# A two-block network on one core: where the 2 KB tiles lie in memory, and how early the first layer's sums of squares are issued

## The chip, the cores and the metric

One core of one Trainium2 chip runs the whole program. The metric is the device time of one execution in microseconds; the runs of the kernel before gave 2714.94 us as their median (2714.61 to 2717.44, 3 runs).

## The reference

The input x has 512 tokens of 1024 features. Two blocks are computed one after the other, both of two layers, all in float32. Cut to what matters:

```python
for l in range(2):                                   # first block
    h = _rmsnorm(x, g_mix[l])                        # over the 1024 features
    p = h @ w_in[l]                                  # 384 + 256 + 32 + 2*512 columns
    ...                                              # latent attention of 8 heads, from p[:, :672]
    a, gt = split(p[..., 672:]); u = a * sigmoid(gt)
    u = silu(layernorm(dwconv31(u)))                 # depthwise, 31 taps, 512 channels
    x = x + concat([y_attn, u]) @ w_o[l]
    z = dwconv3(_rmsnorm(x, g_ffn[l]) @ w_up[l])     # 2 * 2816 columns
    zg, zv = split(z); x = x + (silu(zg) * zv) @ w_down[l]
x = _rmsnorm(x, g_final)
for i in range(2):                                   # second block
    mix = ssd_mixer(x) if i == 0 else hgrn2_mixer(x)
    h = layer_norm(ALPHA * x + mix)
    h = layer_norm(ALPHA * h + relu(h @ mlp_w1[i]) ** 2 @ mlp_w2[i])    # 4096 hidden
    x = h + sigmoid(h @ ple_w_gate[i]) * (p[i] @ ple_w_proj[i])
```

## The kernel before, in words

**Tiling.** Everything is kept with features on the 128 partitions and the 512 tokens along the row, so a float32 tile of [128, 512] is 2 KB in each partition. A dense product is done in float32r with both operands split in a high and a low part: `dense` (L722) issues for each of the 8 blocks of 128 features three matmuls (`mm3`, L717: high x high, high x low, low x high) of 128 x 128 weights with 512 columns of activations (256 where the tokens are cut in halves). Of a matmul's operands the activations are the moving one and the weights the stationary one; all of them are tiles of class s. Weights come from HBM in units of 512 KB to tiles of class r, in the order in which they are used, issued by SP; `weights` (L689) has them split by a cast to the high part (ScalarE or VectorE) and a subtraction to the low part (GpSimd or VectorE). psum has 8 banks of one [128, 512] result each.

**The order.** Nothing is issued while the program is recorded. `Recorder.add` (L408) keeps each operation; `Recorder.schedule` (L464) then places all 19111 of them by a list scheduler with costs of its own, and gives every tile a slot. At each step it takes the operation that can start earliest; between those that can start at once, the smallest `prio` (L481), which is the operation's bias, minus a share of the work behind it, plus its place in the recording. So a bias of 300 lets an operation pass as if it stood 300 places later. The classes of slots and their numbers are in `SLOTS` (L617): 86 of class s, of 2 KB each, 12 of t (512 bytes), 24 of n (up to 128 bytes), 4 of u (2168 bytes at most), 3 of r (4 KB), one each of V (per-channel vectors) and C (constants).

**The addresses.** `Recorder.issue` (L589) goes through the operations in order. The first use of a slot makes a tile in the one SBUF pool (`alloc` in `build`, L1655), and the pool lays tiles one behind the other in the order in which they are made. The first lies at byte 16512 of the partition. Since t, u, n, r, V and C tiles are made between the s tiles, these do not all begin at the same place modulo 512 bytes. In the built program they begin, modulo 512, at

| s tiles | modulo 512 | modulo 256 |
|---|---|---|
| s0 to s22 | 448 | 192 |
| s23 to s44 | 64 | 64 |
| s45, s46 | 96 | 96 |
| s47 to s52 | 128 | 128 |
| s53 | 192 | 192 |
| s54 to s85 | 320 | 64 |

A block of 128 columns of weights in such a tile begins at a multiple of 512 bytes within it.

**The start.** `mixer1` (L905) begins the first layer: `gained` (L773) makes from each of the eight X tiles a high part, scaled (ScalarE), and a low part (VectorE); `sumsq` (L747) squares the same eight tiles (ScalarE) and adds the squares up in two sums (`other`: VectorE or GpSimd); `tok_sum` (L731) adds over the partitions by four matmuls with a column of ones from C; `rstd` (L760) reads that (VectorE) and takes the power -0.5 (GpSimd); `spread` (L767) brings it to all partitions by four transposes, and ScalarE copies it to Rb. Each of the eight products for the convolution is read out of its bank by a multiplication with Rb. The five products of the latents are read without Rb. The bias of the sums is set at L908.

Of the kernel before, what the change touches and what calls it, by code (L numbers as in the profile page):

```python
# [9 lines left out]
F32 = mybir.dt.float32  # L10
# [7 lines left out]
P = 128  # L18
S = 512
# [222 lines left out]
class Ap:  # L242
# [55 lines left out]
    def build(self):  # L298
        x = self.tl.real
        for s in self.steps:  # L300
            if s[0] == "i":
                x = x[s[1]]
            elif s[0] == "r":
                x = x.rearrange(s[1], **s[2])
            elif s[0] == "u":
                x = x.unsqueeze(s[1])
            else:
                x = x.to_broadcast(s[1])
        return x
# [307 lines left out]
SLOTS = {"psum": 8, "r": 3, "s": 86, "u": 4, "t": 12, "n": 24, "V": 1, "C": 1}  # L617
KEEP = {"psum": 2, "s": 18, "u": 2, "t": 6, "n": 16}
SIDE_TAPS = 14
EARLY = 3  # L620
FILL = {"mlp0": [(0, 0)], "mlp1": [(1, 0)]}
FULL = (slice(0, S),)
# [3 lines left out]
def record(R, xT, pos, wts, vecs, consts, pT, outT, dbg=None, stop=None):  # L626
    def tl(shape=(P, S), dt=F32, cls=None):
        b = int(np.prod(shape[1:])) * 4
        cls = cls or ("n" if b <= 128 else "t" if b <= 512 else "s")
        assert cls != "s" or b <= 2048  # L630
        return R.tile(cls, shape, dt)

    def bank():
        return R.tile("psum", (P, S), F32)
# [9 lines left out]
    def vec(name, i=0):  # L644
        o, k = vlay[name]
        return V[:, o + i:o + i + 1]
# [42 lines left out]
    def weights(name, l=None):  # L689

        i = used[0]
        u = units[i]
        assert u[0] == name and (l is None or u[1] == l), (u, name, l)
        used[0] += 1
        c, nk = unit_cols(u), u[3]
        if i not in ahead:
            prefetch(i)
        raw = ahead.pop(i)
        rows, per = [], S // c
        for k in range(0, nk, per):  # L700
            m = min(per, nk - k)
            hi, lo = tl((P, m * c), F32R), tl((P, m * c), F32R)
            src = raw[:, k * c:(k + m) * c]
            copy(hi, src)
            R.either.tensor_sub(lo, src, hi)
            rows += [(hi[:, i * c:(i + 1) * c], lo[:, i * c:(i + 1) * c]) for i in range(m)]
        return rows
# [39 lines left out]
    def sumsq(srcs, sl=slice(0, S), both=True, turned=True):  # L747
        accs = []
        for i, s in enumerate(srcs):
            t = tl()  # L750
            R.scalar.activation(t[:, sl], s[:, sl], AF.Square)
            if i < (2 if both else 1):
                accs.append(t)
            elif both and i % 2:
                R.either.tensor_add(accs[1][:, sl], accs[1][:, sl], t[:, sl])
            else:
                R.other.tensor_add(accs[0][:, sl], accs[0][:, sl], t[:, sl])
        return tok_sum(accs, sl, turned)

    def rstd(ps, n, eps, k=4):  # L760
        v = tl((P, k))
        R.vector.tensor_scalar(v, ps[:, 0:k], 1.0 / n, eps, op0=ALU.mult, op1=ALU.add)
        r = tl((P, k))
        R.gpsimd.tensor_tensor(r, v, nh[:, 0:k], op=ALU.pow)
        return r
# [7 lines left out]
    def gained(name):  # L773

        op = []
        for k in range(KD):
            hi, lo = pair()
            R.scalar.activation(hi, X[k], AF.Identity, scale=vec(name, k))
            R.vector.scalar_tensor_tensor(lo, X[k], vec(name, k), hi, op0=ALU.mult, op1=ALU.subtract)
            op.append((hi, lo))  # L780
        return op
# [123 lines left out]
    def mixer1(l):  # L905
        R.label = f"in{l}"
        op = gained(f"g_mix{l}")
        R.bias = 0  # L908
        r = rstd(sumsq(X, turned=False), D, EPS1)
        R.bias = 0  # L910
        Rb = tl()
# [88 lines left out]
        def conv_tile(j):  # L1000
            R.label, R.bias = f"conv{l}", 100
            acc = bank()
            for k in range(CONV_K - SIDE_TAPS):
                wc = vec(f"w_dw_conv{l}", j * CONV_K + k)
# [4 lines left out]
            side = None  # L1009
            for k in range(CONV_K - SIDE_TAPS, CONV_K):  # L1010
                t = tl()
# [141 lines left out]
    def ssd(op):  # L1153
# [69 lines left out]
        def inputs(g):  # L1223
# [3 lines left out]
            if g == 0:  # L1227
                ws, ps = [weights("ssd_w_in_2") for _ in range(EARLY)], [bank() for _ in range(EARLY)]
                for sl in HALVES:
# [404 lines left out]
    for l in range(DEPTH):  # L1634
        mixer1(l)
        dump(f"mix{l}", X)
        if stop == f"mix{l}":
            return
        op = ffn1(l)
        dump(f"ffn{l}" if l == 0 else "b1", X)  # L1640
        if stop == f"ffn{l}":
            return
# [12 lines left out]
def build(tc, xT, pos, wts, vecs, consts, pT, outT, dbg=None, stop=None):  # L1655
    R = Recorder()
    record(R, xT, pos, wts, vecs, consts, pT, outT, dbg, stop)
    R.schedule(SLOTS, KEEP)
    with tc.manual_schedule(), tc.tile_pool(name="sbuf", bufs=1) as sb, \
            tc.tile_pool(name="psum", bufs=1, space=bass.MemoryType.PSUM) as ps:  # L1660
        
        def alloc(t):
            pool = ps if t.cls == "psum" else sb
            name = f"{t.cls}{t.slot}"
            return pool.tile(list(t.shape), t.dt, tag=name, name=name, bufs=1)
        R.issue(tc.nc, alloc)
    return R

# [28 lines left out]
```

## Time and profile before

| | |
|---|---|
| median of 3 runs | 2714.94 us |
| profiled execution, its own time | 2715.32 us |
| span of the profiled execution | 2713.5 us |
| mean granted TensorE clock | 0.993 |
| busy: TensorE, its weight loads | 98%, 82% |
| busy: VectorE, ScalarE, GpSimd | 70%, 44%, 31% |
| moved from HBM | 230 MB |

The span goes from the first to the last instruction; the execution's own time has 1.8 us more around it. In the rows PE is TensorE's matmul, PEld its weight load, DVE VectorE, ACT ScalarE, POOL GpSimd, SP the engine that issues the DMAs. A matmul's busy time is its life in the pipeline, and lives overlap: the step from one to the next is told by starts. All recorded operations have one line (L599, in `issue`), so that rows are told apart by tiles; buffer numbers are left out of them.

### The profile page before, as it was taken

How to read it: one execution, taken by the hardware profiler on the slowest of the kernel's cores; microseconds unless marked ns; L12 is line 12 of the kernel's file. 1: busy time of each engine (PE TensorE's matmuls, PEld its weight loads, DVE VectorE, ACT ScalarE, POOL GpSimd, SP SyncE). 2: the span in 40 equal slices, each digit the busy share in tenths (PEclk: the TensorE clock that was granted, in tenths of full speed). 3: DMA queues.
4: the chain of work that ended last, by engine and by line, in shares of the span. 5: the costliest groups of instructions: out<-in, count | busy, mean ns of one | idle time of the engine just before them, and what ended most of it. 6: DMA issues, size and time to landing. Idle time of an engine off the chain costs nothing.

```text
span 2713.5 us, 38992 instructions
## 1 busy us (share of the span) xinstructions
PE 2671.4 (98%) x15094; PEld 2212.1 (82%) x15094; DVE 1898.9 (70%) x3222; ACT 1200.9 (44%) x2206; POOL 834.2 (31%) x691
## 2 busy tenths in 40 slices
PE   9999999999999999999999999999999999999999
PEld 7777888888778888888778888888988789888889
DVE  8997676678976666685887675555688787554546
ACT  5874333346764323343664432222367674322223
POOL 3561011235721111232441432232412233223332
PEclk8999999999999999999999999999999999999999
DMA  4123132230131223321113412232231123322320
GB/s 164 35 71 116 63 112 98 101 109 29 59 112 62 86 93 109 110 80 63 51 36 109 148 55 103 87 106 97 73 105 48 64 74 107 107 100 89 109 94 32
DMA packets 69449, 235.00 MB, mean 87 GB/s; under 512 B 7824, under 2 KB 11152, under 8 KB 69264
## 3 DMA queue, kind: packets, MB, share of 16 engines
q1 hardware_dynamic: 69264, 232.51, 25.3%
q8 instruction: 119, 1.95, 0.3%
q14 instruction: 66, 0.54, 0.1%
HBM read 230.38 MB, written 2.10 MB: 86 GB/s over the span
## 4 chain that ended last, share of the span: by engine, by line
PE 91%; DVE 6%; issue 1%; ACT 1%; POOL 0%; DMA 0%; SPq 0%; POOLq 0%; ACTq 0%; DVEq 0%
PE psum L599 91%; DVE s L599 5%; DVE psum L599 1%; ACT s L599 1%; DVE n L599 0%; POOL s L599 0%; DMA s<-xT 0%; DVE u L599 0%; SPq L599 0%; POOLq L599 0%; ACTq L599 0%; DVEq L599 0%
## 5 line engine op out<-in xcount | busy, mean ns | idle before, releaser
L599 PE MATMUL psum<-s,s 128*128 128x512 f32 (+4 forms) x12992 | 2608.2, 365 | 23.9 <-DVE s L599 14.7
L599 PEld LDWEIGHTS psum<-s,s 128*128 128x128 f32 (+2 forms) x12992 | 2116.1, 185 | 459.7 <-issue 23.2
L599 POOL TENSOR_TENSOR s<-r,s 128x512 fp32r<-128x512 f32 (+1 forms) x363 | 502.8, 1400 | 1092.5 <-ACT s L599 819.7
L599 ACT CAST s<-r 128x512 fp32r<-128x512 f32 (+1 forms) x743 | 420.6, 612 | 386.4 <-DMA r<-wts 375.4
L599 DVE TENSOR_TENSOR s<-s,s 128x512 f32<-128x512 f32 (+5 forms) x605 | 415.1, 707 | 68.4 <-ACT s L599 57.6
L599 POOL TENSOR_TENSOR s<-s,s 128x512 f32<-128x512 f32 (+5 forms) x234 | 273.0, 1179 | 539.9 <-ACT s L599 290.4
L599 DVE TENSOR_TENSOR s<-s,psum 128x512 f32<-128x512 f32 (+2 forms) x400 | 225.3, 591 | 266.9 <-PE psum L599 265.3
L599 DVE TENSOR_TENSOR s<-r,s 128x512 fp32r<-128x512 f32 x506 | 401.6, 820 | 5.3 <-ACT s L599 2.7
L599 ACT ACTIVATE s<-s 128x512 f32<-128x512 f32 (+1 forms) x335 | 186.2, 578 | 243.7 <-DVE s L599 240.2
L599 ACT ACTIVATE s<-u,V 128x512 f32<-128x512 f32 x200 | 143.0, 761 | 270.4 <-DVE u L599 270.0
L599 ACT ACTIVATE s<-psum 128x512 f32<-128x512 f32 (+2 forms) x176 | 91.9, 524 | 344.5 <-PE psum L599 342.6
L599 DVE SCALAR_TENSOR_TENSOR s<-u,V,s 128x512 f32<-128x512 f32 x176 | 145.9, 830 | 49.0 <-ACT s L599 47.2
L599 DVE SCALAR_TENSOR_TENSOR s<-psum,s 128x512 f32<-128x512 f32 (+1 forms) x88 | 55.7, 640 | 105.0 <-ACT s L599 104.7
L599 DVE TENSOR_TENSOR u<-psum,s 128x512 f32<-128x512 f32 x88 | 60.7, 690 | 92.3 <-PE psum L599 90.3
L599 ACT COPY s<-psum 128x512 f32<-128x512 f32 (+5 forms) x162 | 76.0, 503 | 79.2 <-PE psum L599 77.8
L599 ACT CAST s<-s 128x512 fp32r<-128x512 f32 (+2 forms) x123 | 72.0, 591 | 74.7 <-DVE s L599 67.5
L599 ACT ACT_TABLE_LOAD x72 | 92.4, 1283 | 8.7 <-DVE s L599 6.8
L599 DVE SCALAR_TENSOR_TENSOR psum<-u,V,psum 128x512 f32<-128x512 f32 x128 | 91.8, 743 | 0.3
L599 PE MATMUL psum<-C,s 128*128 128x128 f32 (+1 forms) x532 | 84.9, 272 | 4.5 <-ACT s L599 3.0
L599 DVE SCALAR_TENSOR_TENSOR s<-psum,V,s 128x511 f32<-128x511 f32 (+4 forms) x90 | 65.5, 743 | 29.8 <-ACT s L599 20.7
L599 PEld LDWEIGHTS psum<-C,s 128*128 128x128 f32 x532 | 67.3, 150 | 20.0 <-ACT s L599 7.2
L599 DVE CAST s<-r 128x512 fp32r<-128x512 f32 (+1 forms) x126 | 56.0, 455 | 39.0 <-DMA r<-wts 38.1
(87 smaller groups left out, 834.7 us busy)
## 6 DMA issues: line engine op xcount, KB each, us to landing
r<-wts SPq DMA_DIRECT2D x415, 512.0 KB, 3.5
r<-wts SPq DMA_DIRECT2D x12, 256.0 KB, 2.6
r<-wts SPq DMA_DIRECT2D x8, 384.0 KB, 3.0
s<-xT SPq DMA_DIRECT2D x8, 256.0 KB, 6.1
s<-pT SPq DMA_DIRECT2D x8, 256.0 KB, 3.0
outT<-s SPq DMA_DIRECT2D x16, 128.0 KB, 1.8
r<-wts SPq DMA_DIRECT2D x9, 128.0 KB, 2.0
V<-vecs SPq DMA_DIRECT2D x1, 479.0 KB, 6.7
```

What stands on the lines that cost most here:

```text
L599: getattr(eng, meth)(*[res(a) for a in args], **{k: res(v) for k, v in kw.items()})
```

## The change

It does two things. Before anything is issued, `build` makes all 86 s tiles one behind the other, after a pad of 480 bytes, so that the first begins at 16992 and all of them at 96 modulo 512 (and 96 modulo 256). The other classes come behind them. And in the first layer the sums of squares in front of the mixer are recorded with a bias of 300 in place of 0.

```diff
--- before.py
+++ after.py
@@ -617,6 +617,7 @@
 SLOTS = {"psum": 8, "r": 3, "s": 86, "u": 4, "t": 12, "n": 24, "V": 1, "C": 1}
 KEEP = {"psum": 2, "s": 18, "u": 2, "t": 6, "n": 16}
 SIDE_TAPS = 14
+FIRST = 16512
 EARLY = 3
 FILL = {"mlp0": [(0, 0)], "mlp1": [(1, 0)]}
 FULL = (slice(0, S),)
@@ -905,7 +906,7 @@
     def mixer1(l):
         R.label = f"in{l}"
         op = gained(f"g_mix{l}")
-        R.bias = 0
+        R.bias = 300 if l == 0 else 0
         r = rstd(sumsq(X, turned=False), D, EPS1)
         R.bias = 0
         Rb = tl()
@@ -1663,6 +1664,12 @@
             pool = ps if t.cls == "psum" else sb
             name = f"{t.cls}{t.slot}"
             return pool.tile(list(t.shape), t.dt, tag=name, name=name, bufs=1)
+
+        pad = (96 - FIRST) % 512
+        if pad:
+            sb.tile([P, pad // 4], F32, tag="pad", name="pad", bufs=1)
+        for n in range(SLOTS["s"]):
+            sb.tile([P, S], F32, tag=f"s{n}", name=f"s{n}", bufs=1)
         R.issue(tc.nc, alloc)
     return R
 
```

Where the instructions stand: the schedule differs in the first layer's mixer and what surrounds it; from within the first layer's feed-forward part on, the operations stand in the same order on every engine, in other slots. The names below have the slot ahead of the underscore; the numbers behind it count tiles as they are made, and differ between the two programs.

VectorE at the start, where the low parts of X (SCALAR_TENSOR_TENSOR with V) and the adds of squares (TENSOR_TENSOR of s and s) are made; before:

```order
L599 SCALAR_TENSOR_TENSOR s19_144<-s6_114,V0_65,s16_138 128x512
L599 TENSOR_TENSOR s4_110<-s4_110,s18_142 128x512
L599 TENSOR_TENSOR s14_134<-s14_134,s21_149 128x512
L599 SCALAR_TENSOR_TENSOR s24_164<-s8_118,V0_65,s22_153 128x512
L599 TENSOR_TENSOR s4_110<-s4_110,s23_159 128x512
L599 TENSOR_TENSOR s14_134<-s14_134,s25_166 128x512
L599 SCALAR_TENSOR_TENSOR s29_180<-s10_125,V0_65,s26_169 128x512
L599 TENSOR_TENSOR s14_134<-s14_134,s27_174 128x512
L599 TENSOR_TENSOR s4_110<-s4_110,s28_178 128x512
```

and now:

```order
L599 SCALAR_TENSOR_TENSOR s17_227<-s6_201,V0_152,s14_221 128x512
L599 SCALAR_TENSOR_TENSOR s22_240<-s8_205,V0_152,s19_232 128x512
L599 SCALAR_TENSOR_TENSOR s24_247<-s10_212,V0_152,s21_237 128x512
L599 SCALAR_TENSOR_TENSOR s26_256<-s12_217,V0_152,s23_245 128x512
L599 SCALAR_TENSOR_TENSOR s28_263<-s15_223,V0_152,s25_251 128x512
L599 SCALAR_TENSOR_TENSOR s30_271<-s18_230,V0_152,s27_259 128x512
L599 TENSOR_TENSOR s16_225<-s16_225,s29_266 128x512
L599 SCALAR_TENSOR_TENSOR s33_283<-s20_234,V0_152,s31_273 128x512
L599 CAST s36_292<-r1_253 128x512
```

The adds that stood between the low parts stand behind six of them, one by one, and among the splits of weights.

TensorE, around the four matmuls with the column of ones from C that sum the squares over the partitions; these are rows 16 to 20 before:

```order
L599 MATMUL psum1_122<-s30_182,s13_132 128x512
L599 MATMUL psum1_122<-s31_188,s11_128 128x512
L599 MATMUL psum2_211<-C0_155,s4_110 128x1 x4
L599 MATMUL psum3_222<-s3_108,s36_209 128x512
L599 MATMUL psum3_222<-s5_112,s36_209 128x512
```

and rows 144 to 148 now:

```order
L599 MATMUL psum6_459<-s33_283,s56_388 128x512
L599 MATMUL psum6_459<-s31_273,s59_402 128x512
L599 MATMUL psum7_579<-C0_243,s4_197 128x1 x4
L599 MATMUL psum0_593<-s3_195,s58_400 128x512
L599 MATMUL psum0_593<-s5_199,s58_400 128x512
```

The sums went from row 18 to row 146, behind all 24 matmuls of the first six products (psum1 to psum6). VectorE's reading of them went from row 25 of its order to row 72, and the four transposes that spread the result from TensorE's row 36 to row 159.

TensorE, rows 187 to 196 before (the moving tile is the first behind the arrow, the weights the second):

```order
L599 MATMUL psum1_503<-s31_188,s73_390 128x512
L599 MATMUL psum5_471<-s43_235,s66_352 128x512
L599 MATMUL psum1_503<-s32_193,s71_381 128x512
L599 MATMUL psum5_471<-s34_199,s68_364 128x512
L599 MATMUL psum1_503<-s39_219,s71_381 128x512
L599 MATMUL psum1_503<-s32_193,s73_390 128x512
L599 MATMUL psum1_503<-s34_199,s71_381 128x512
L599 MATMUL psum1_503<-s43_235,s71_381 128x512
L599 MATMUL psum1_503<-s34_199,s73_390 128x512
L599 MATMUL psum3_639<-s3_108,s74_395 128x512
```

and now:

```order
L599 MATMUL psum7_637<-s25_251,s66_434 128x512
L599 MATMUL psum0_593<-s33_283,s60_406 128x512
L599 MATMUL psum7_637<-s27_259,s64_423 128x512
L599 MATMUL psum0_593<-s31_273,s62_416 128x512
L599 MATMUL psum7_637<-s30_271,s64_423 128x512
L599 MATMUL psum7_637<-s27_259,s66_434 128x512
L599 MATMUL psum7_637<-s31_273,s64_423 128x512
L599 MATMUL psum7_637<-s33_283,s64_423 128x512
L599 MATMUL psum7_637<-s31_273,s66_434 128x512
L599 MATMUL psum1_702<-s3_195,s68_449 128x512
```

The same products stand there in other slots: those before lie at 64 modulo 256 except s3 of the last row, at 192; those now lie at 96.

## Rows read from the trace of the kernel before

**Rows 1.** The page: busy times, TensorE's clock in 40 slices, the chain that ended last.
```profile
PE 2671.4 (98%) x15094; PEld 2212.1 (82%) x15094; DVE 1898.9 (70%) x3222; ACT 1200.9 (44%) x2206; POOL 834.2 (31%) x691
...
PEclk8999999999999999999999999999999999999999
...
PE 91%; DVE 6%; issue 1%; ACT 1%; POOL 0%; DMA 0%; SPq 0%; POOLq 0%; ACTq 0%; DVEq 0%
```

**Rows 2.** Groups by shape: busy us, mean ns of one | idle before, releasers.
```profile
L599 PE MATMUL psum<-s,s 128*128 128x512 f32 x9200 | 2256.7, 398 | 10.4 <-DVE s L599 6.2 <-ACT s L599 2.4 <-issue 1.6
...
L599 PE MATMUL psum<-s,s 128*128 128x256 f32 x2640 | 377.0, 283 | 6.1 <-DVE s L599 4.9 <-ACT s L599 1.1
...
L599 DVE TENSOR_TENSOR s<-s,psum 128x512 f32<-128x512 f32 x256 | 170.3, 683 | 243.6 <-PE psum L599 242.3 <-POOL s L599 0.4
...
L599 PE MATMUL psum<-C,s 128*128 128x128 f32 x464 | 75.4, 276 | 3.3 <-ACT s L599 3.0
```

**Rows 3.** Three stretches: length, then each engine's busy us (starts); clock; DMA share, GB/s.
```profile
300.00:600.00 300.00, 300.00 (x1298) 243.56 (x1297) 203.57 (x286) 101.48 (x168) 62.42 (x51) 1.00 0.30 104
1650.00:1900.00 250.00, 250.00 (x1083) 202.97 (x1083) 129.60 (x167) 62.07 (x111) 69.25 (x50) 1.00 0.27 97
2350.00:2580.00 230.00, 230.00 (x997) 186.81 (x996) 113.75 (x138) 54.43 (x99) 74.64 (x54) 1.00 0.28 99
```

**Rows 4.** TensorE's timeline in four stretches: start us, length us, equal instructions merged.
```profile
54.19 7.43 PE L599 MATMUL psum<-s,s 128*128 128x512 f32 x32
...
50.54 10.85 PE L599 MATMUL psum<-s,s 128*128 128x512 f32 x47
...
44.74 7.56 PE L599 MATMUL psum<-s,s 128*128 128x512 f32 x32
...
327.90 7.86 PE L599 MATMUL psum<-s,s 128*128 128x512 f32 x33
```

**Rows 5.** Two stretches of 6.8 us: busy us of each engine (starts).
```profile
54.43:61.23 6.80, 6.80 (x32) 5.63 (x30) 6.80 (x8) 3.40 (x6) 6.56 (x6) 1.00 0.01 3
2450.00:2456.80 6.80, 6.80 (x31) 5.57 (x31) 1.37 (x2) 0.00 (x0) 1.95 (x2) 1.00 0.21 77
```

**Rows 6.** TensorE's timeline from 1035.9 to 1039.5 us.
```profile
1035.65 4.05 PE L599 MATMUL psum<-s,s 128*128 128x512 f32 x17
```

**Rows 7.** TensorE's timeline, 256 columns, near 2313 us and from 2677 us.
```profile
2312.45 1.96 PE L599 MATMUL psum<-s,s 128*128 128x256 f32 x15
...
2677.05 32.26 PE L599 MATMUL psum<-s,s 128*128 128x256 f32 x271
```

**Rows 8.** The timeline of all engines from 8.66 to 25.2 us.
```profile
10.67 1.13 ACT L599 ACTIVATE s<-s 128x512 f32<-128x512 f32 x2
...
11.46 1.29 DVE L599 TENSOR_TENSOR s<-s,s 128x512 f32<-128x512 f32 x2
...
18.52 0.16 DVE L599 TENSOR_SCALAR n<-psum 128x4 f32<-128x4 f32 x1
...
18.83 1.34 POOL L599 TENSOR_TENSOR n<-n,n 128x4 f32<-128x4 f32 x1 [16.69 <-DVE n L599]
...
24.17 0.60 PE L599 MATMUL psum<-C,n 128*128 128x128 f32 x4
...
24.80 0.59 ACT L599 COPY s<-psum 128x512 f32<-128x512 f32 x1 [5.53 <-PE psum L599]
```

**Rows 9.** Stretches of the start: busy us of each engine (starts).
```profile
0.00:8.66 8.66, 6.15 (x26) 5.19 (x26) 3.60 (x10) 4.07 (x6) 1.57 (x14) 1.00 0.71 234
8.66:22.32 13.66, 12.54 (x30) 8.20 (x30) 13.20 (x25) 10.38 (x19) 1.34 (x1) 0.50 0.73 259
```

**Rows 10.** GpSimd's timeline from 16 to 60 us.
```profile
28.04 1.30 POOL L599 TENSOR_TENSOR s<-r,s 128x512 fp32r<-128x512 f32 x1 [7.86 <-ACT s L599]
...
51.15 9.48 POOL L599 TENSOR_TENSOR s<-s,s 128x512 f32<-128x512 f32 x5 [8.44 <-ACT s L599]
```

**Rows 11.** One stretch, the mixer of the first layer.
```profile
40.00:210.00 170.00, 165.99 (x849) 128.19 (x848) 164.76 (x244) 122.65 (x241) 109.02 (x89) 0.99 0.19 64
```

## Prediction

> **What bounds the kernel now.** I read the page first, then the groups of instructions by shape, then equal stretches, and last TensorE's own timeline, since only there one sees the step from one matmul to the next. The page: TensorE is busy 98% of the span, at full clock in all slices but the first, and 91% of the chain that ended last is TensorE on psum [rows 1]. So outside a few waits the time is the number of matmuls times the step between their starts. The groups give the number: 9200 matmuls of 512 columns and 2640 of 256, from s tiles into psum, beside short ones with the constants tile C [rows 2]. The mean of 398 ns there is the pipelined life of one, not the step. The step is in the stretches: 1298 starts in 300 us, 1083 in 250 and 997 in 230, which is 231.1, 230.8 and 230.7 ns, with VectorE at 68%, 52% and 49% [rows 3]. At 2.4 GHz 512 columns are 213 ns, so some 18 ns of each step are neither columns nor waiting.
>
> **The step isn't a constant.** In the timeline, a row of n matmuls lasts (n - 1) steps and one life of 0.398 us. The 32 in 54.19 to 61.62 us give (7.43 - 0.398)/31 = 226.8 ns, the 47 from 50.54 us on 227.2; 32 from 44.74 us on 231.0; 33 at 328 us 233.2 [rows 4]. What is different? Not the neighbours: in the fastest stretch VectorE and GpSimd are busy 6.80 and 6.56 us of 6.80, while at 2450 us they are busy 1.37 and 1.95 and fit a matmul fewer into the same 6.80 us [rows 5]. It is the addresses. The fast row is PE's rows 166 to 195 of the order, nine of which are shown above: moving tiles of s26 to s43, weight tiles of s59 to s73. By the addresses given above, every one of these begins at 64 modulo 256 bytes (64 or 320 modulo 512). The next matmul in the order takes s3 (448 modulo 512, so 192 modulo 256) with s74 (64), and the step is broken. In the stretches at 231 ns s0 to s22 (192), s47 to s52 (128) and the 64s come mixed. I take it that the step is shortest when the moving tile and the weights, of this matmul and of its neighbours, have equal residues, and that a difference costs several ns each time it appears. It takes a while to settle: 17 matmuls at 1035.65 us, which come out of a mixed stretch, give (4.05 - 0.398)/16 = 228.3 ns [rows 6].
>
> For 256 columns it is the other way round, and smaller: 15 matmuls of equal residue give (1.96 - 0.283)/14 = 119.8 ns, and 271 in the mixed end (32.26 - 0.283)/270 = 118.4 [rows 7].
>
> **The change part by part.** *The addresses.* After the change all 86 s tiles begin at 96 modulo 512, and pieces of weights begin at multiples of 512 bytes in a tile, so nearly all of these matmuls have equal residues all the time. No instruction is added by this. The step of the 512-column matmuls goes from 231.1 to 226.8 ns: 9200 x 4.3 = 39.6 us. I count it where TensorE ends the time, 91%: 36 us. Off that come 3 us for settling: 1.5 ns over 16 matmuls is 0.024 us a break, and the 464 transposes by C [rows 2], in groups of four and more, make up to 116 breaks. That leaves -33 us. The 256-column ones cost 2640 x 1.4 x 0.91 = +3.4 us. The bounds of this term: no saving at all, as the trace has no stretch whose operands are all at 96; and 39.6 - 3.4 = 36 us if every matmul is on the path. I take it near the upper end, because it is nearest to the measured row of equal residues; what I carry over is that equality counts and not the value 64. Other engines read the same tiles, but are not on the path in these stretches [rows 3].
>
> *The order.* Only the sums of squares in front of the first mixer move, and what queues behind them. Before, ScalarE alternates squares (1.13 us for two) and scaled copies, VectorE low parts and adds (1.29 for two), so that the operands of a matmul wait for squares too [rows 8]; TensorE is busy 6.15 of the first 8.66 us and 12.54 of the next 13.66, these at half clock [rows 9]. In the changed order the low parts come first, so the first unit is fed up to 4 us earlier (seven squares of 0.57 us). TensorE takes this as 3.6 us less idling at best. Against it: the matmuls that sum over partitions stand at row 146, not 18, with 24 matmuls of each of six units ahead; VectorE reads them at row 72, not 25. The eight projections of the convolution need their result, and six of eight banks hold such products by then. GpSimd's rsqrt stands ahead of all its other work, so the eight operations that it did from 28 to 61 us (the first and the last row of them: [rows 10]) slip behind some 50 us, where the convolution begins later too. That stage is VectorE's: 164.8 of 170 us busy from 40 to 210, GpSimd 109.0 [rows 11]. What GpSimd can't catch up falls to VectorE at 0.68 us for an add [rows 2]: at most 8 x 0.68 = 5.4 us, and once a wait for the chain of read, rsqrt, spread and copy, 0.16 + 1.34 + 0.60 + 0.59 = 2.7 us [rows 8]. So this part lies between -4 and +8; I take +3, a little over the middle, because VectorE's busy time is the row nearest to the end of that stage, and GpSimd's lost start comes out of it. SP's queue keeps its order but for one load of positions that lets a load of weights pass; ScalarE's five copies fewer have room.
>
> The sum: -33 + 3 + 3 = -27 from the profiled execution's 2715.3 (span 2713.5 and 1.8 around it), which stands 0.4 us over the median: **2688 us**.
>
> **The rivals.** *Addresses don't matter* (0.12). The fast row would then be chance, or belong to its place in the program. For it: there is just one such long row at 226.8, and rows of 12 or 15 elsewhere are mixed with settling. Against: the step is the same to 0.1 ns over 31 matmuls, and VectorE or GpSimd can't make it. Time: 2715.3 + 3 = 2718. The Trainium skill speaks for this rival: "TensorE: Matmul & The Clock Gate", section "Back-to-back issue gap", has the step from columns and clock alone, 518 cycles at 512 columns, and "SBUF — State Buffer", section "Who interferes with whom", gives TensorE two independent read ports and says that it never waits on anyone. By 518 cycles, an estimate of 216 ns, every step here would be shorter than any that the trace shows, so the trace disagrees with the first already.
>
> *Half of it* (0.17). 96 is a multiple of 32 and not of 64, unlike 64, 128 and 192, so the step may settle above 226.8; or the weights and other forms break it more often than I count. Half of the saving: 2715.3 - 16.5 + 1.5 + 3 = 2703.
>
> *Slower* (0.09). If a start at an odd multiple of 32 costs each matmul a step more in reading its 2 KB, equal residues don't help. The price is that of the slowest rows, 233.2 ns [rows 4]: 9200 x 2.1 x 0.91 = 17.6 us, and the order's 3: 2736. It decides as soon as the settled step lies above 231.5. Against it: s45 and s46 stand at 96 now, and no stretch with them is beyond 233.3.
>
> **How the numbers follow.** My forecast has 0.62, with 2680 to 2700 of its own (the order's -4 to +8, and some us of settling). The range of 2677 to 2715 holds it, the half case, and the lower end of the first rival. A measurement of this kernel tells 0.2%, 5.4 us, from no change. Faster by more, below 2709.5: 0.62 + 0.14 = 0.76. Within: 0.03 of the half case and 0.08 of the first rival, 0.11. Slower: 0.04 of the first rival and 0.09, 0.13.
>
> **What would show it.** Right: the stretches of rows 3 hold 2% more starts, near 227 ns each, and long timeline rows of 512 columns all over the program give 226.7 to 227; 256 columns near 120; the mixer stage of the first layer ends about where it did; the squares are done after the low parts, the half clock begins at the same place and ends sooner, and a gap of TensorE at 50 to 55 us is new. Wrong: 231 in the same stretches (first rival), one steady value between (half), above 231.5 (slower). If the step is 226.8 and the span is not below 2700, the saving was taken by waits, which would show as idle time of TensorE behind VectorE or ScalarE in the stretches from 1200 to 1400 and 1930 to 2250 us.

## The result and the profile after

| | before | changed |
|---|---|---|
| median | 2715.99 us (4 runs, 2714.61 to 2717.44) | 2685.26 us (4 runs, 2681.69 to 2686.31) |
| ratio, 95% interval | | 0.9884 [0.9867, 0.9902] |
| span of the profiled execution | 2713.5 us | 2684.2 us |

The changed kernel is 30.7 us faster; 2688 had been forecast, 27 us less than before. The page of the changed kernel, beside [rows 1]:

```profile
PE 2638.4 (98%) x15094; PEld 2212.4 (82%) x15094; DVE 1896.3 (71%) x3225; ACT 1198.4 (45%) x2201; POOL 829.2 (31%) x693
...
PEclk9999999999999999999999999999999999999999
...
PE 91%; DVE 6%; issue 1%; ACT 1%; POOL 1%; DMA 0%; SPq 0%; POOLq 0%; ACTq 0%; DVEq 0%
```

The same 15094 matmuls, TensorE still 98% busy and 91% of the chain, VectorE with three instructions more and 2.6 us less: nothing was taken away, and nothing took TensorE's place as the bound. The two large groups of matmuls, beside [rows 2]:

```profile
L599 PE MATMUL psum<-s,s 128*128 128x512 f32 x9200 | 2219.9, 395 | 13.2 <-DVE s L599 8.9 <-ACT s L599 2.7 <-issue 1.3
...
L599 PE MATMUL psum<-s,s 128*128 128x256 f32 x2640 | 380.3, 284 | 5.7 <-DVE s L599 4.6 <-ACT s L599 1.1
```

The counts are the same. A group's mean is the life of one in the pipeline, so the change shows there little. It shows in the stretches (length, each engine's busy us with its starts, clock, DMA share, GB/s), beside [rows 3]:

```profile
300.00:600.00 300.00, 300.00 (x1326) 248.48 (x1325) 207.98 (x294) 107.71 (x178) 66.37 (x53) 1.00 0.30 104
1650.00:1900.00 250.00, 250.00 (x1105) 207.07 (x1104) 133.13 (x165) 67.45 (x123) 86.15 (x63) 1.00 0.30 106
2350.00:2580.00 230.00, 230.00 (x1017) 190.50 (x1016) 121.36 (x150) 58.03 (x106) 70.96 (x52) 1.00 0.29 100
```

In the same 300, 250 and 230 us there are 28, 22 and 20 starts more: 226.2 ns from one to the next in place of 231.1 in the first. TensorE's timeline of one long stretch (start, length, equal instructions merged), first before, then after:

```profile
1034.72 65.48 PE L599 MATMUL psum<-s,s 128*128 128x512 f32 x283
```

```profile
1034.81 65.44 PE L599 MATMUL psum<-s,s 128*128 128x512 f32 x288
...
2647.40 32.75 PE L599 MATMUL psum<-s,s 128*128 128x256 f32 x271
```

By the rule of the prediction, (length - 0.398)/(n - 1), that is 230.8 and 226.6 ns: five matmuls more in the same 65 us. The last stretch of 256 columns went the other way, from 118.4 [rows 7] to (32.75 - 0.284)/270 = 120.2 ns.

**Where the time went, in full.** I took the start of every matmul from the trace and summed the differences by kind of pair. From the first to the last matmul: 2708.0 us before and 2678.8 now. Pairs of 512 columns: 2038.6 and 2001.1, so -37.5. Pairs of 256 columns: 276.4 and 279.6, so +3.1. All others (short matmuls, changes of shape): 393.0 and 398.2, so +5.2. Of the -37.5, steps under 250 ns account for 33.7 to 33.9 (some 8350 pairs, whose mean fell from 231.21 to 227.15 ns), and the rest lies in some 290 longer pairs, which hold waits and matmuls at half clock.

### The profile page after: what moved, and what is told of

It reads as the page before. It is cut to its first block, busy times and chain, and to the rows that moved or that the text cites. A ratio compares the mean times of both kernels' runs of the same rounds, so it can differ in the third digit from the quotient of the medians.

```text
span 2684.2 us, 38981 instructions
## 1 busy us (share of the span) xinstructions
PE 2638.4 (98%) x15094; PEld 2212.4 (82%) x15094; DVE 1896.3 (71%) x3225; ACT 1198.4 (45%) x2201; POOL 829.2 (31%) x693
## 4 chain that ended last, share of the span: by engine, by line
PE 91%; DVE 6%; issue 1%; ACT 1%; POOL 1%; DMA 0%; SPq 0%; POOLq 0%; ACTq 0%; DVEq 0%
PE psum L599 91%; DVE s L599 4%; DVE psum L599 1%; ACT s L599 1%; POOL s L599 1%; DVE n L599 0%; DMA s<-xT 0%; DVE u L599 0%; SPq L599 0%; POOL n L599 0%; POOLq L599 0%; ACTq L599 0%; DVEq L599 0%
## 5 line engine op out<-in xcount | busy, mean ns | idle before, releaser
L599 PE MATMUL psum<-s,s 128*128 128x512 f32 (+4 forms) x12992 | 2574.3, 362 | 25.9 <-DVE s L599 17.0
L599 POOL TENSOR_TENSOR s<-r,s 128x512 fp32r<-128x512 f32 (+1 forms) x366 | 509.9, 1409 | 1078.3 <-ACT s L599 820.1
L599 DVE TENSOR_TENSOR s<-s,s 128x512 f32<-128x512 f32 (+4 forms) x607 | 417.4, 708 | 69.0 <-ACT s L599 58.2
L599 POOL TENSOR_TENSOR s<-s,s 128x512 f32<-128x512 f32 (+4 forms) x232 | 264.6, 1153 | 505.0 <-ACT s L599 234.4
L599 DVE TENSOR_TENSOR s<-r,s 128x512 fp32r<-128x512 f32 (+1 forms) x503 | 389.5, 800 | 6.3 <-ACT s L599 3.9
L599 POOL TENSOR_TENSOR n<-n,n 128x4 f32<-128x4 f32 (+1 forms) x32 | 35.1, 1095 | 160.2 <-DVE n L599 159.8
```

The source lines that it names most:

```text
L599: getattr(eng, meth)(*[res(a) for a in args], **{k: res(v) for k, v in kw.items()})
```

## The experiments

Two columns of the table behind them are counted as above: the mean step of 512 columns (pairs under 250 ns, 8340 to 8370 of them in each kernel) and of 256 columns (pairs under 140 ns, some 2220). Where a time is marked (one), it is that of one execution.

**The two halves of the change, apart.** addr_only takes the bias back and keeps the addresses:

```diff
-        R.bias = 300 if l == 0 else 0
+        R.bias = 0
```

> The s tiles side by side at 96 modulo 512 as in the change, but the sums of squares in their old place in the order. Theory A (the addresses make the whole gain; the shift of the sums costs little): mean step of 512-column matmuls near 227 ns, 256-column ones near 119.5 ns, time 30 to 34 us under before, 2682 to 2686. Rival B (the new order makes the gain): 231 ns and 2712 to 2718.

Measured: 2687.28 us (4 runs), 1.3 us above what theory A had offered, ratio to before 0.9889 [0.9874, 0.9905], steps of 227.17 and 119.53 ns. old_offsets keeps the changed order, and puts the tiles back to where they began modulo 512:

```diff
-        pad = (96 - FIRST) % 512
+        pad = (448 - FIRST) % 512
...
+        gaps = {23: 128, 45: 32, 47: 32, 53: 64, 54: 128}
         for n in range(SLOTS["s"]):
+            if n in gaps:
+                sb.tile([P, gaps[n] // 4], F32, tag=f"gap{n}", name=f"gap{n}", bufs=1)
             sb.tile([P, S], F32, tag=f"s{n}", name=f"s{n}", bufs=1)
```

> The changed order, and the s tiles still made first and one behind the other, but with five small gaps between them, so that each begins at the residue modulo 512 that it had before (448, 64, 96, 128, 192, 320). Theory A: step 231 ns again, 256 columns 118.1 ns, time within 4 us of before, 2712 to 2719; what differs is the order's price alone, which I put at +3. Rival B (order), and rival C (that the tiles lie together, not where they begin): 2685 and 227 ns.

Measured: 2714.20 us (11 runs), ratio 0.9991 [0.9982, 1.0000], 231.33 and 118.20 ns. The same long stretch in both, addr_only first:

```profile
1034.77 65.44 PE L599 MATMUL psum<-s,s 128*128 128x512 f32 x288
```

```profile
1034.71 65.55 PE L599 MATMUL psum<-s,s 128*128 128x512 f32 x283
```

226.6 and 231.0 ns. So the addresses make nearly the whole gain, and neither the order nor the mere fact that the tiles lie together makes it. The order alone is worth some 2 us, and to the better, where I had expected 3 us to the worse. These 2 us are at the edge of the noise: the interval of old_offsets reaches up to 1.0000, and the four runs of addr_only spread over 5 us.

**Must moving tile and weights be equal, or only each constant?** In the changed kernel both hold. roles128 keeps each constant and makes them unequal: a pass behind the scheduler deals the slots out again, 34 for tiles that are only weights, 52 for the rest, and a gap of 128 bytes stands between the groups.

```diff
+    def regroup(self, nw, total):
...
+                    g = "W" if role.get(id(t)) == {"W"} else "M"
+                    if not free[g]:
+                        g = "M" if g == "W" else "W"
+                    free[g].sort()
+                    slot[id(t)] = t.slot = free[g].pop(0)[1]
...
     R.schedule(SLOTS, KEEP)
+    R.regroup(34, SLOTS["s"])
...
+            if n == SLOTS["s"] - 34:
+                sb.tile([P, 32], F32, tag="gap", name="gap", bufs=1)
```

> The changed kernel with the slots dealt out by role behind the scheduler: 34 slots for tiles that are only weights, 52 for all others, and a gap of 128 bytes between the two groups. So 8625 of 9212 matmuls of 512 columns take moving tiles at 96 and weights at 224 modulo 256, and 8445 have the same pair of residues as the one before. Theory A1, that of the prediction (moving tile and weights must have equal residues): 231 ns or more, 2712 to 2725. Rival A2 (each of the two only has to stay at one residue from one matmul to the next; what they are to each other doesn't count): 227 to 227.5 ns, 2685 to 2690. Rival A3 (moving and weights that differ collide less): under 226.5 ns, 2680 or less.

Measured: 2738.71 us (4 runs), ratio 1.0081 [1.0067, 1.0095], slower than before, and 14 us beyond what A1 had offered. Its control has the same slots without the gap, and roles64 a gap of 64 (one execution each):

> The same slots by role without any gap: all tiles at 96. It holds the slots' part of roles128 alone. A1: 227 ns, and only the waits that the other choice of slots brings, 2685 to 2697 (the matmuls other than the long ones took 10 us more in roles128 than in the changed kernel). Rival (the slots by role, not the 128 bytes, made roles128 slow): 232 ns and 2730 or more.

> As roles128, with a gap of 64 bytes: moving tiles at 96, weights at 160 modulo 256, in nearly all matmuls. A1 (equal modulo 256 is what counts, any difference costs the same): 232 to 233 ns for 512 columns as with 128 bytes, 2730 to 2742. A1b (the cost depends on the distance): another steady value between 226.6 and 241, and below 226.6 if some distance suits the reads better than none: 2670 or less.

roles0: 2698.48 us and 227.14 ns, so dealing the slots out by role costs 13 us, of which I followed only that most of them lie in pairs other than the long ones; the gap of 128 bytes costs the other 40. roles64: 2739.16 us. The same stretch, without a gap, with 128 and with 64 bytes:

```profile
1034.63 65.67 PE L623 MATMUL psum<-s,s 128*128 128x512 f32 x289
```

```profile
1034.77 65.46 PE L623 MATMUL psum<-s,s 128*128 128x512 f32 x281
```

```profile
1034.69 65.50 PE L623 MATMUL psum<-s,s 128*128 128x512 f32 x280
```

226.6, 232.4 and 233.3 ns. Rivals A2 and A3 fall: with both constant and unequal the step is longer than in the mixture before. It doesn't settle to one value there either: in roles64 the starts of that stretch lie 231 and 236 ns apart by turns, in the changed kernel 226 or 227.

**Does the distance count, and its sign?** Gaps of 192 and of 32 bytes (one execution each):

> Slots by role as in roles128 and roles64, with a gap of 192 bytes: weights lie 192 bytes ahead of the moving tile modulo 256, which is 64 behind it (288 modulo 512, 32 modulo 256). If only the distance counts, whichever of the two is ahead: 233.2 ns as in roles64, 2739. If the sign counts: another value; and under 226.6 ns, 2690 or less, if the reads of this pair fall between each other. A1 has no gain anywhere, so 231 ns or more.

> The same with a gap of 32 bytes: moving tiles at 96, weights at 128 modulo 256. If any inequality costs: 231 to 234 ns, 2732 to 2742. If the two need only lie in the same 64 bytes, or the cost grows with the distance: 227 to 230 ns, 2698 to 2720. The control of both is roles0 with 2698.

```profile
1034.79 65.40 PE L623 MATMUL psum<-s,s 128*128 128x512 f32 x285
```

```profile
1034.68 65.50 PE L623 MATMUL psum<-s,s 128*128 128x512 f32 x280
```

228.9 and 233.3 ns, in times 2710.72 and 2739.00 us, against 2698.48 without a gap. So 32 bytes cost as much as 64: that the cost grows with the distance, or that the two need only lie in the same 64 bytes, is wrong. 192 (the weights 64 behind, by residue) costs 2.2 ns, where 64 ahead costs 5.9 (means of the table below, against roles0), so the sign counts, as the second rule for roles192 had it, but without the gain that was held possible. The rule of the distance alone missed, and so did A1, which had 231 ns or more for any difference. Of the distances tried (32, 64, 128 and 192) none is better than zero.

**Is 96 a good place, and is 256 the period?** at128 moves all the tiles on by 32 bytes:

```diff
-        pad = (96 - FIRST) % 512
+        pad = (128 - FIRST) % 512
```

> The changed kernel with all s tiles at 128 modulo 512 in place of 96, a multiple of 128 bytes. A1 (only equality counts, not the place): 227.1 ns, 2682 to 2690. Rival (a start that is a multiple of 64 or 128 bytes reads faster than an odd multiple of 32): 224 to 226 ns, 2660 to 2676; or slower, if 96 was a good place: 229 ns and more, 2700.

And in split128 and split256 one gap, of 128 and of 256 bytes, stands ahead of s23:

```diff
+            if n == 23:
+                sb.tile([P, 32], F32, tag="gap", name="gap", bufs=1)
```

> The changed kernel with one gap of 128 bytes ahead of s23: tiles at 96 and at 224 modulo 256, mixed in both roles (moving and weights equal in 6420 of 9212 matmuls, the same pair as the one before in 4755). Theory A1 and A2: residues differ again, step 229.5 to 231 ns, time 2700 to 2715. Rival C (that the tiles lie together): 227 ns and 2685.

> The gap ahead of s23 is 256 bytes in place of 128: tiles at 96 and at 352 modulo 512, mixed, all at 96 modulo 256. A1 with 256 bytes as the period: 227 ns, 2682 to 2690. Rival (the period is 512 bytes or more): as split128, 230.4 ns and 2700 to 2711.

split128: 2707.73 us (5 runs), ratio 0.9967 [0.9955, 0.9979], 230.40 ns. split256: 2684.61 us, 227.16 ns. at128: 2684.42 us, 227.14 ns. The stretch in at128 and in split256:

```profile
1034.71 65.67 PE L599 MATMUL psum<-s,s 128*128 128x512 f32 x289
```

```profile
1034.69 65.67 PE L599 MATMUL psum<-s,s 128*128 128x512 f32 x289
```

226.6 ns in both. So the place doesn't count (96 or 128), and residues modulo 256 are enough; those modulo 512 needn't agree.

| kernel | moving, weights modulo 256 | 512 columns | 256 columns | time, us |
|---|---|---|---|---|
| before | mixed | 231.21 | 118.14 | 2715.99 |
| old_offsets | mixed as before | 231.33 | 118.20 | 2714.20 |
| split128 | 96 and 224, mixed | 230.40 | 118.40 | 2707.73 |
| changed | 96, 96 | 227.15 | 119.54 | 2685.26 |
| addr_only | 96, 96 | 227.17 | 119.53 | 2687.28 |
| split256 | 96, 96 | 227.16 | 119.55 | 2684.61 (one) |
| at128 | 128, 128 | 227.14 | 119.55 | 2684.42 (one) |
| roles0 | 96, 96, slots by role | 227.14 | 119.56 | 2698.48 (one) |
| roles192 | 96, 32 | 229.33 | 117.58 | 2710.72 (one) |
| roles128 | 96, 224 | 232.43 | 118.79 | 2738.71 |
| roles64 | 96, 160 | 233.08 | 117.40 | 2739.16 (one) |
| roles32 | 96, 128 | 233.13 | 118.22 | 2739.00 (one) |

**What the order gives, and what it gives back.** The four transposes that spread the factor ahead of the first layer's feed-forward part are a mark that every kernel passes. Its rows in TensorE's timeline, for the kernel before, old_offsets, addr_only and the changed one:

```profile
247.39 0.60 PE L599 MATMUL psum<-C,n 128*128 128x128 f32 x4
```

```profile
243.18 0.60 PE L599 MATMUL psum<-C,n 128*128 128x128 f32 x4
```

```profile
248.05 0.60 PE L599 MATMUL psum<-C,n 128*128 128x128 f32 x4
```

```profile
246.59 0.60 PE L599 MATMUL psum<-C,n 128*128 128x128 f32 x4
```

With the old addresses the new order reaches the mark 4.2 us earlier, with the new ones 1.5 us. (In these 250 us the addresses by themselves bring nothing in these two executions, 247.39 and 248.05: in this stage VectorE is busy some 225 of the 250 us.) By single matmuls, addr_only against the changed kernel (times are those of addr_only): the changed one is 5.9 us ahead at matmul 300, 9.0 at 400 (102 us) and 9.7 at 420 (107 us), but 1.4 at 480 (120 us); then 3.1 at 650, 0.3 at 700 (161 us), 2.9 behind at 900 (194 us), and 1.8 ahead at 1132. So the early start is real, and more than all of it is given back between 100 and 200 us, some 8 us of it by 120 us. The stretch from 100 to 120 us in addr_only, the changed kernel and old_offsets:

```profile
100.00:120.00 20.00, 19.55 (x94) 15.42 (x93) 19.61 (x30) 15.35 (x30) 14.87 (x11) 1.00 0.08 26
```

```profile
100.00:120.00 20.00, 16.09 (x57) 11.29 (x56) 17.43 (x23) 14.25 (x31) 14.07 (x11) 0.83 0.01 2
```

```profile
100.00:120.00 20.00, 15.66 (x72) 11.13 (x71) 19.46 (x27) 15.55 (x33) 15.34 (x12) 1.00 0.01 2
```

In both kernels with the new order TensorE idles some 4 us there, behind VectorE and ScalarE; in the changed one the granted clock falls to half behind these waits as well (0.83 on average), and 57 matmuls start in place of 94. Farther on, one wait stands out. The changed kernel's timeline there has these rows of VectorE, GpSimd and TensorE:

```profile
144.71 1.28 POOL L599 TENSOR_TENSOR s<-r,s 128x512 fp32r<-128x512 f32 x1
...
145.35 8.29 DVE L599 CAST s<-s 128x512 fp32r<-128x512 f32 x1
...
145.95 7.40 POOL L599 TENSOR_TENSOR s<-s,s 128x512 f32<-128x512 f32 x6
...
153.78 1.42 PE L599 MATMUL psum<-s,s 128*128 128x512 f32 x2 [4.40 <-DVE s L599]
```

One cast on VectorE lasts from 145.35 to 153.64 us, while GpSimd does a subtraction and six adds one behind the other, up to 153.35; TensorE idles 4.40 us behind VectorE. A cast of this shape takes 0.41 us where nothing holds it (the row of bias100 below). In the kernel before, one of the same shape came when more of such a row of GpSimd's was done, and lasted 4.96 us:

```profile
144.49 7.45 POOL L599 TENSOR_TENSOR s<-s,s 64x512 fp32r<-64x512 f32 x6 [1.06 <-ACT s L599]
...
147.27 4.96 DVE L599 CAST s<-s 128x512 fp32r<-128x512 f32 x1
```

The Trainium skill has a rule for this, "SBUF — State Buffer", section "Who interferes with whom": VectorE's second pair of ports is GpSimd's only one, a cast can take both pairs, and whoever comes second is blocked entirely. The trace agrees: in both kernels GpSimd was already running when the cast came, and the cast ends 0.29 us behind the last of GpSimd's row (153.64 and 153.35; 152.23 and 151.94). So the cast found no way in between adds that stand one behind the other; no run here tried a pause between them.

The changed kernel so loses 3.3 us more in this one cast than the kernel before. It is the smaller part of what is given back: its lead over addr_only falls by 2.8 us around it, and by 8.3 from matmul 420 to 480. And old_offsets, which has the same order and no cast held there (one tensor_tensor of VectorE's takes 4.25 us), falls back as far against the kernel before, from 8.7 us ahead at matmul 400 to 0.3 at 900. If it is the late sums that push GpSimd's work together there, an earlier place should help, and bias100 puts them there:

```diff
-        R.bias = 300 if l == 0 else 0
+        R.bias = 100 if l == 0 else 0
```

> The changed kernel with a bias of 100 in place of 300, so that TensorE's sums over the partitions stand at row 65 of its order, between row 27 (bias 0 with the new addresses) and row 155 of the recorder's count. Steps as in the changed kernel, 227 ns. The order by itself has been worth 1.8 us to the end of the first layer's feed-forward start (the new order against the old one at equal addresses): 5.9 us gained by 67 us, and 4 given back from 100 to 200 us. If the giving back is due to the late sums (Rb late, products waiting in their banks, GpSimd idle), an earlier place keeps more of the gain: 2679 to 2684. If it is due to VectorE's work in the mixer, which no order shortens: 2684 to 2687.

Measured: 2680.35 us (4 runs), ratio 0.9868 [0.9852, 0.9885]. The mark, and the group of such casts from 120 to 160 us (busy us, mean ns of one):

```profile
237.77 0.60 PE L599 MATMUL psum<-C,n 128*128 128x128 f32 x4
```

```profile
L599 DVE CAST s<-s 128x512 fp32r<-128x512 f32 x1 | 0.4, 409 | 0.0
```

The mark is 8.8 us earlier than in the changed kernel, and no cast is held from 120 to 160 us. The interval overlaps the changed kernel's, so it was made again, with the place that at128 had shown to be as good:

> The bias of 100 again, with all s tiles at 128 modulo 512, which at128 showed to step like 96. If the 4 to 5 us that bias100 had over the changed kernel come from the order, they are here again: 2678 to 2683. If they were an accident of those executions: 2683 to 2687, as the changed kernel, at128 and split256.

Measured: 2678.50 us (4 runs, 2677.33 to 2679.40), ratio 0.9864 [0.9847, 0.9880], the mark at 237.99 us. All eight runs of the two lie at 2677.3 to 2682.6, and the four of the changed kernel, at128 and split256 at 2681.7 to 2686.3. So a bias of 100 is some 5 us better than 300, and this version has the lowest median of all. What makes these 5 us is not shown. The held cast was not taken away by itself, bias100 moves other work too, and there is a rival that no run tests, TensorE's clock. The first 250 us in the kernel before, the changed one, at128, old_offsets and bias100:

```profile
0.00:250.00 250.00, 240.20 (x1141) 186.39 (x1142) 224.24 (x351) 168.22 (x316) 121.51 (x110) 0.96 0.29 98
```

```profile
0.00:250.00 250.00, 237.40 (x1145) 186.73 (x1146) 224.22 (x355) 167.69 (x312) 118.82 (x112) 0.96 0.29 98
```

```profile
0.00:250.00 250.00, 236.97 (x1154) 186.29 (x1155) 227.00 (x358) 167.53 (x313) 118.63 (x112) 0.98 0.31 98
```

```profile
0.00:250.00 250.00, 237.41 (x1160) 183.33 (x1161) 225.69 (x359) 167.80 (x313) 120.91 (x112) 1.00 0.30 99
```

```profile
0.00:250.00 250.00, 241.01 (x1182) 189.80 (x1183) 225.81 (x361) 171.68 (x321) 124.74 (x113) 0.99 0.32 101
```

The mean granted clock of 0.96 in the changed kernel is 20.5 us at half clock, the 0.99 of bias100 is 3.4 us. Half of the difference, 8.5 us, is an estimate of the most that it can cost, and nearly the whole lead at the mark. At128 shows the same from another side: with the changed kernel's order and step, 10.2 us at half clock and a cast held just as long, its mark is 2.0 us earlier:

```profile
244.62 0.60 PE L599 MATMUL psum<-C,n 128*128 128x128 f32 x4
```

Two of the changed kernel's three stretches at half clock begin in or just behind TensorE's waits (110.6 and 151.6 us), so the clock may be a part of what the waits cost, and not a cause beside them; no run takes them apart.

## Why the prediction was right, point by point

**The step at equal residues** was forecast at 226.8 ns from one long row [rows 4], and is 227.15 on average, 226.6 in a long stretch. The term of -33 came out as -33.7 to -33.9. Each of the two corrections in it was about right: the steps counted above are some 8350 for 9200 matmuls, 0.91, and settling took some 3.8 us where 3 were forecast (in the changed kernel the steps more than fifteen matmuls behind another shape are 226.7 ns on average; the mean of 227.15 lies 0.45 above that, times 8350).

**What counts** was taken to be equality of moving tile and weights modulo 256, and not the value 64. addr_only, at128, split256 and roles128 bear this out. The part of it that was too strong is that every difference costs alike: the distance and its sign matter. That the neighbours count too shows when the starts in the trace are set beside the order and the addresses of the built program. In the kernel before, 4958 of 9188 matmuls did have equal residues, yet the step came to 231. The first step of a sequence that keeps one equal pair is 230.8 ns, the fifth 229.7, and from the eleventh on 226.7 (split128 gets there as late); only some 70 of 8240 steps are that far into one. An equal pair at another residue than the equal one before it is no better than a break: 231.0 ns, 279 of them. So equal residues pay only where they last. What in the chip makes the difference stays open.

**256 columns**: +3.4 forecast, +3.1 measured.

**The order**: +3 forecast, about -2 measured (-1.5 to -4.2 at the mark, -2.0 and -1.8 between medians of separate groups of runs). The bounds of -4 to +8 held it, and the sign was wrong. The step that failed is that what GpSimd loses at the start would fall to VectorE at 0.68 us an add. It didn't: in the first 250 us VectorE is busy 224.24 us before and 224.22 now (the rows above), and over the whole program it has three instructions more and GpSimd two. The first three stretches of the start, beside [rows 9], and TensorE's row from 48 us on:

```profile
0.00:8.66 8.66, 5.70 (x26) 4.85 (x26) 3.34 (x10) 3.66 (x6) 1.57 (x14) 0.98 0.65 204
8.66:15.00 6.34, 6.34 (x14) 4.60 (x15) 5.88 (x10) 6.34 (x11) 0.00 (x0) 0.50 1.03 398
15.00:22.32 7.32, 7.32 (x33) 5.98 (x33) 7.32 (x15) 3.22 (x7) 0.00 (x0) 1.00 0.83 276
...
47.96 14.33 PE L599 MATMUL psum<-s,s 128*128 128x512 f32 x62
```

The half clock begins where it did and ends near 15 us rather than 22.3, as forecast; the starts from 8.66 to 22.32 us, some 46 against 30, are the early gain. The gap that I expected at 50 to 55 us isn't there: TensorE does 62 matmuls without a break from 47.96 us. What takes back the gain is waits of TensorE behind VectorE and ScalarE and the half clock beside them, the larger part from 100 to 120 us; the held cast is one of these waits.

**The rivals.** That addresses don't matter falls with the kernels of one order that differ in addresses alone (before and addr_only; the changed kernel, old_offsets, at128 and the two splits; roles0 and the four with gaps); the rule that the prediction cited for it, columns and clock alone ("TensorE: Matmul & The Clock Gate", section "Back-to-back issue gap", of the Trainium skill; the section calls its 518 cycles the gap of an isolated matmul), has no place for steps of 226.6 to 233.3 ns at the same 512 columns and full clock. The half case, as far as it rested on 96 being an odd multiple of 32, and the slower one fall with at128, which steps like 96; the other reason of the half case, more breaks than counted, came to the settling above. Yet the step of that one, 233.2 ns, is what unequal residues cost when they are held all the time (roles32, roles64); that their 2739 us lie so near to its 2736 is chance, since 13 us of them are the price of the slots by role.

**The sum.** In the traces the shorter steps make -33.8 us, the pairs of 256 columns +3.1, the longer pairs of 512 columns -3.7 and the pairs of other shapes +5.2, together -29.2; the medians differ by 30.7. The address terms of the prediction, -33 and +3.4, stand in this nearly as forecast. The order's term is in the last two, mixed with all other waits, and no run takes these apart. The forecast of -27 missed by 3.7 us: the order's term was some 5 us off, and some 2 us that stay open went the other way.

## What to carry to other kernels

When TensorE is the bound and its busy share is already near 100%, look at the step between starts and not at the busy share: a step that differs from stretch to stretch, at one shape and one clock, is time that may be had. Moving tiles and weights that begin at one residue modulo 256 bytes were worth 1.1% here, with no instruction changed; it is a matter of which tiles a pool lays out first. They were worth it because all tiles had that residue: a sequence broken every few matmuls gained little. An early start in one stage is worth only what the next stage doesn't give back: look there for TensorE's waits and for its granted clock, and not only for the engine that is busy.

## What the runs showed that I had not expected

- Three of the four constant but unequal pairs are worse than a mixture: 232.4 ns at 128 bytes, 233.3 at 32 and 64, against 230.8 in the same stretch before. The sign counts: 233.3 with the weights 64 ahead, 228.9 with them 64 behind (192). Distances of 96, 160 and 224 weren't tried.
- At 256 columns equality is the slowest of all: 119.56 ns, against 117.40 to 118.79 for the four other pairs. By these numbers a kernel with such matmuls alone would want the tiles apart, which no run tried; what makes the two lengths differ is open.
- With the low parts first the clock stayed up longer at the start. The same stretch in addr_only (sums early), old_offsets and bias100 (low parts first):

```profile
8.66:22.32 13.66, 11.71 (x29) 7.78 (x30) 12.91 (x22) 10.72 (x20) 1.34 (x1) 0.59 0.72 262
```

```profile
8.66:22.32 13.66, 12.89 (x53) 9.61 (x53) 13.30 (x24) 8.94 (x17) 0.00 (x0) 1.00 0.90 321
```

```profile
8.66:22.32 13.66, 12.61 (x50) 9.07 (x51) 12.92 (x23) 9.60 (x17) 0.00 (x0) 1.00 0.78 286
```

TensorE's granted clock is 0.59 with 29 starts in the one, 1.00 with 53 and 50 in the others; before it was 0.50 with 30 [rows 9], in the changed kernel 0.77. All kernels with low parts first lie at 0.77 or more. That the better fed start is the reason is likely, but not shown: the starts and the clock rise together. How much of what the order gains at the mark is the clock's (4.2 us in old_offsets, which has none at half clock up to there; 1.5 in the changed kernel, which has 20.5 us) I can't tell apart.
